# Adding four partial sums of squares on VectorE before the variance product, in two of four layer norms

## The chip, the cores and the metric

One NeuronCore of one Trainium2 chip runs the whole kernel. The metric is the device time of one execution, in microseconds (us), and a kernel is judged by the median of its runs. TensorE (PE in the profile) multiplies matrices, VectorE (DVE) and ScalarE (ACT) do elementwise work, GpSimd (POOL) and SyncE (SP) issue the data transfers (DMA) here.

## The reference

The kernel computes a trunk of two layers on an input of 512 tokens by 1024 features, all in float32. Layer 0 mixes tokens by a state-space group and an attention group; layer 1 by a convolution. Each layer ends as follows:

```python
x = layer_norm(DEEPNORM_ALPHA * x + mix, ln1_g[layer], ln1_b[layer])
ffn = sqrelu_mlp(x, ffn_w1[layer], ffn_b1[layer], ffn_w2[layer], ffn_b2[layer])
x = layer_norm(DEEPNORM_ALPHA * x + ffn, ln2_g[layer], ln2_b[layer])
```

A layer norm takes, for each token, the mean of its 1024 features and the mean of the squared differences from it:

```python
mu = jnp.mean(xf, axis=-1, keepdims=True)
var = jnp.mean(jnp.square(xf - mu), axis=-1, keepdims=True)
y = (xf - mu) * lax.rsqrt(var + LN_EPS)
```

The convolution of layer 1 has a further layer norm inside it.

## The kernel before

**Layout.** The activations lie transposed: features on the 128 partitions, tokens along the free dimension. The 1024 features make eight tiles (`KT = 8`) of 128 x 512. A product in nearly full float32 precision is made of three matmuls on split operands: each tensor is kept as a high part and a low part (`whi` and `wlo` for weights, `xbh` and `xbl` for the activations behind norm "b"), and `gemm` (its matmuls are recorded as L256) multiplies high by high, high by low and low by high for each of eight tiles, so 24 matmuls make one output tile.

**The layer norms.** Four norms are made in this way: "a" behind the mixer of layer 0, "b" behind the first FFN, "c" inside the convolution, "d" behind the convolution. (The last norm of the kernel is made differently.) Each works on two halves of the tokens, 256 columns each, since `HALVES` is (0, 256) and (256, 512). Since the features lie on partitions, a sum over features crosses partitions; TensorE does that in `colmean`, by a matmul whose stationary operand is the constant tile `ones` (recorded as L954). Its operands are plain float32. `centre` subtracts the mean from the eight tiles (VectorE, L385), squares them (ScalarE, L185) into eight tiles `sq`, and adds neighbours on VectorE (L385), so that four partial sums are left; `scale` passes these four to `colmean`, which accumulates four matmuls in one PSUM tile, named `vpb` for norm "b" and `vpd` for norm "d" (`mpb` and `mpd` hold the mean). `rsqrt` then takes the reciprocal square root on ScalarE (L191) and improves it in three VectorE operations (`tb`, `tb`, `rb`). `ln_to_x` multiplies each tile by the result and splits it into `xbh` and `xbl`.

**What covers the norms.** `tail_norm_lead` interleaves the norm with other products so that TensorE has work. The tail is the last product before the norm, eight output tiles for each half (PSUM tiles `tlb`, `tld`). The lead is the first product behind the norm (PSUM tiles `pl` behind norm "b" and `fl` behind norm "d"). By `BEFORE = (1, 3, 1, 2)`, the first half has one tail tile of the second half ahead of its mean product and three more ahead of its variance product; the second half has one lead tile (on the first half's result) ahead of its mean product and two more ahead of its variance product. Behind norm "b" the lead has four tiles, behind norm "d" six. When the lead has been made on the first half, `Lead.finish` makes it on the second half, which needs the second half's `xbh` and `xbl`.

**What sets the order.** The Tile framework's scheduler places instructions from the program's order and its own costs; `colmean` uses `tc.issue_after(last)`, so that its matmuls are placed behind the last matmul of the covering product. On each engine the instructions then run strictly in that order. Weights of the leads come from DRAM copies that were kept earlier (`kepth`, `keptl`), loaded by DMAs that GpSimd issues.

Of the kernel before, what the change touches and what calls it, by code (L numbers as in the profile page):

```python
# [13 lines left out]
ALU = mybir.AluOpType  # L14
# [29 lines left out]
LEAD = 6  # L44
TOGETHER = {'fl1': 2}
LN_ON_V = "abcd"
KEEP_FROM = 8
AHEAD = (5, 4)
FJ = 3
# [109 lines left out]
def units_of(name, w, k0, nk, cols, width):  # L159

    ncol = 1024 // nk
    out = []
    for c in cols:
        base = c // width * width
        src = w[k0 * P : (k0 + nk) * P, base : base + width].rearrange("(k p) n -> p k n", p=P)
        out.append(((name, k0, base), src, nk, ncol, c - base, width))
    return out
# [29 lines left out]
def kernel(ctx: ExitStack, tc: tile.TileContext, a: dict, out: bass.AP):  # L197
# [186 lines left out]
    def tt(o, x, y, op):  # L384
        V.tensor_tensor(o, x, y, op=op)  # L385
        return o
# [493 lines left out]
    def tmp(name, dt=F32):  # L880
        return hid.tile([P, T], dt, tag="tmp", name=name, bufs=8)
# [14 lines left out]
    for layer in range(2):  # L896
# [4 lines left out]
        for nb in FFN_BLOCKS[layer]:  # L901
# [11 lines left out]
            for m in range(k0, k0 + nb, 4):  # L913
                units += units_of("f10", a["ffn_w1"][0], 0, 8, range(m * P, min(m + 4, k0 + nb) * P, 128), 256)
                if m >= KEEP_FROM:
                    keep_at["f", m + 3] = kept[n : n + 2]
# [14 lines left out]
    class LN:  # L931
# [29 lines left out]
        def centre(self, ys, c0, c1, other=None):  # L961

            mu = self.colmean([self.s[c0]], c0, c1, "m", other)
            sq = []
            for j, y in enumerate(ys):
                tt(y[:, c0:c1], y[:, c0:c1], mu, ALU.subtract)
                sq.append(tmp(f"sq{self.n}{c0}{j}")[:, c0:c1])
                act(sq[j], y[:, c0:c1], AF.Square)
            for j in range(0, KT, 2):
                tt(sq[j], sq[j], sq[j + 1], ALU.add)  # L970
            return sq[::2]

        def scale(self, sq, c0, c1, other=None):
            var = self.colmean(sq, c0, c1, "v", other)
# [531 lines left out]
```

## Time and profile before

| what | value |
|---|---|
| median of 3 runs | 1173.91 us (1172.56 to 1175.39) |
| the profiled execution | 1172.98 us |
| its span, first to last instruction | 1171.2 us |
| mean granted TensorE clock | 0.993 |
| TensorE busy with matmuls | 1138.9 us (97%) |
| VectorE busy | 822.9 us (70%) |
| ScalarE busy | 551.7 us (47%) |

Norm "b" lies at about 597 to 639 us of the span, norm "d" at about 788 to 831 us. One float32 matmul of `colmean` is recorded as two matmul instructions, so a variance product of four shows as "x8". Busy times of TensorE overlap, because a matmul is recorded until its last result is out while the next has begun; what a group of matmuls takes is read from the chain of waits, which follows back from the last instruction what released each piece of work and counts no time twice.

### The profile page before, as it was taken

Reading aid. Unit: us, or ns where it says so; the run is one execution under the profiler, and the core shown is the slowest. Engines: PE = TensorE matmul, PEld = TensorE weight load, DVE = VectorE, ACT = ScalarE, POOL = GpSimd, SP = SyncE. Lnnn points to the kernel's source line nnn. Section 1 sums busy time; section 2 is a strip of 40 time slices with the busy share of each in tenths; the row PEclk is TensorE's granted clock in tenths of the full one; section 3 lists DMA queues with packets and bytes.
Section 4 is the critical chain, followed back from the end, with each engine's and each line's share of the span. In section 5 each row is a group of like instructions: output and inputs, shape, how many; then the busy total and the mean of one; then the engine's idle time right before and its main releaser. Section 6 shows DMA issues by size and latency. Waiting matters only on the chain.

```text
span 1171.2 us, 17896 instructions
## 1 busy us (share of the span) xinstructions
PE 1138.9 (97%) x7180; PEld 953.1 (81%) x7180; DVE 822.9 (70%) x1396; ACT 551.7 (47%) x838; POOL 67.0 (6%) x125
## 2 busy tenths in 40 slices
PE   9989999999999999999999999899989999999997
PEld 7777767799888888888999777599968888887885
DVE  7999875498646546546555899886785958587337
ACT  7857779345425425425323132662753536363530
POOL 1022210000000000000021110001000000000000
PEclk9999999999999999999999999999989999999999
DMA  8521221332688788788454742206324151514211
GB/s 216 165 56 50 79 85 46 110 116 73 221 286 289 250 287 290 249 286 286 164 177 152 247 144 74 75 9 209 91 79 138 56 151 37 170 36 153 63 55 72
DMA packets 145907, 169.59 MB, mean 145 GB/s; under 512 B 13922, under 2 KB 119138, under 8 KB 145824
## 3 DMA queue, kind: packets, MB, share of 16 engines
q1 hardware_dynamic: 137024, 136.96, 36.7%
q0 software_dynamic: 8640, 31.46, 7.9%
q8 instruction: 56, 0.92, 0.3%
q14 instruction: 27, 0.22, 0.1%
q10 hardware_dynamic: 160, 0.03, 0.0%
HBM read 132.12 MB, written 35.65 MB: 143 GB/s over the span
## 4 chain that ended last, share of the span: by engine, by line
PE 82%; DVE 9%; ACT 4%; issue 2%; DMA 2%; POOL 0%; SPq 0%; DVEq 0%; ACTq 0%; POOLq 0%
PE f L256 24%; PE acf L256 11%; PE s L1390 8%; PE fl L256 5%; PE tlb L256 4%; PE tld L256 4%; PE h L1436 4%; PE pv L256 3%; PE pg L256 3%; PE cw L1165 3%; PE tla L256 2%; PE acmo L256 2%; PE pl L256 2%; DVE wlo L111 1%; PE gg L256 1%
## 5 line engine op out<-in xcount | busy, mean ns | idle before, releaser
L110 ACT CAST whi<-raw 128x1024 fp32r<-128x1024 f32 (+1 forms) x150 | 156.7, 1061 | 257.9 <-PE acf L256 61.0
L111 DVE TENSOR_TENSOR wlo<-raw,whi 128x1024 fp32r<-128x1024 f32 (+1 forms) x150 | 183.8, 1238 | 123.9 <-ACT whi L110 120.5
L256 PE MATMUL f<-xdh,whi 128*128 128x512 f32 x208 | 81.0, 390 | 1.0 <-ACT whi L110 1.0
L256 PE MATMUL f<-xah,whi 128*128 128x512 f32 x208 | 81.1, 390 | 0.0
L256 PE MATMUL f<-xal,whi 128*128 128x512 f32 x208 | 80.9, 389 | 0.0
L256 PE MATMUL f<-xah,wlo 128*128 128x512 f32 x208 | 80.9, 389 | 0.0
L256 PE MATMUL f<-xdl,whi 128*128 128x512 f32 x208 | 80.9, 389 | 0.0
L256 PE MATMUL f<-xdh,wlo 128*128 128x512 f32 x208 | 80.9, 389 | 0.0
L256 PE MATMUL acf<-hh,whi 128*128 128x512 f32 x192 | 75.4, 392 | 0.0
L256 PE MATMUL acf<-hh,wlo 128*128 128x512 f32 x192 | 75.2, 392 | 0.0
L256 PE MATMUL acf<-hl,whi 128*128 128x512 f32 x192 | 74.8, 390 | 0.0
L1390 PE MATMUL s<-whi,ah 128*128 128x512 f32 x168 | 66.0, 400 | 3.3 <-ACT whi L110 2.5
L1390 PE MATMUL s<-wlo,ah 128*128 128x512 f32 x168 | 66.4, 402 | 2.3 <-DVE wlo L111 2.3
L1390 PE MATMUL s<-whi,al 128*128 128x512 f32 x168 | 66.0, 396 | 0.0
L111 DVE TENSOR_TENSOR wlo<-quad,whi 128x1536 fp32r<-128x1536 f32 x28 | 49.0, 1754 | 4.7 <-ACT whi L110 4.4
L110 ACT CAST whi<-quad 128x1536 fp32r<-128x1536 f32 x28 | 41.0, 1478 | 21.9 <-PE f L256 8.0
L389 DVE SCALAR_TENSOR_TENSOR cy<-hp,wdw,cy 128x512 f32<-128x512 f32 (+1 forms) x75 | 49.5, 660 | 0.2 <-ACT cy L185 0.2
L95 POOL DMA_DIRECT2D whi<-kepth x30 | 16.1, 536 | 547.7 <-PE tlb L256 385.5
L256 PEld LDWEIGHTS f<-xdh,whi 128*128 128x128 f32 x208 | 39.0, 188 | 9.4 <-ACT whi L110 1.4
L256 PEld LDWEIGHTS f<-xah,whi 128*128 128x128 f32 x208 | 39.0, 188 | 8.2
L256 PEld LDWEIGHTS f<-xdh,wlo 128*128 128x128 f32 x208 | 39.0, 188 | 8.2
L256 PEld LDWEIGHTS f<-xah,wlo 128*128 128x128 f32 x208 | 39.0, 188 | 8.1
(649 smaller groups left out, 3069.1 us busy)
## 6 DMA issues: line engine op xcount, KB each, us to landing
raw<-in_ffn_w_dram SPq DMA_DIRECT2D x35, 1024.0 KB, 5.6
kepth<-whi SPq DMA_DIRECT2D x30, 512.0 KB, 3.4
keptl<-wlo SPq DMA_DIRECT2D x30, 512.0 KB, 9.4
whi<-kepth POOLq DMA_DIRECT2D x30, 512.0 KB, 3.6
wlo<-keptl POOLq DMA_DIRECT2D x30, 512.0 KB, 4.6
raw<-in_ffn_w_dram SPq DMA_DIRECT2D x28, 512.0 KB, 4.1
raw<-in_conv_w_pw_dram SPq DMA_DIRECT2D x12, 1024.0 KB, 7.3
quad<-in_ffn_w_dram SPq DMA_DIRECT2D x16, 768.0 KB, 4.8
```

The costliest lines, as they stand in the source:

```text
L95: nc.gpsimd.dma_start(x, d)
L110: i0 = nc.scalar.copy(hi, raw).ins
L111: i1 = nc.vector.tensor_sub(lo, raw, hi.bitcast(F32)).ins
L256: ins = PE.matmul(ps[:, c0:c1], u[:, k, ksl], v[:, c0:c1], start=start and k == 0 and i == 0, stop=stop and k == n - 1 and i == 2).ins
L389: V.scalar_tensor_tensor(o, x, s, y, op0=op0, op1=op1)
L1165: PE.matmul(cps[j, c0][g][C, :], Ds[j][t // 16][R, t % 16, :], hps[j][R, t + c0 : t + c1], start=t < 4, stop=t >= n - 4, tile_position=(R. ...
L1390: PE.matmul(ps, u, v[:, p, :], start=chain == i and p == 0 and n_ == 0, stop=p == len(As) - 1 and n_ == 2, skip_group_check=True)
L1436: PE.matmul(ps, u, v, start=k == 0 and i == 0, stop=k == nb_last - 1 and i == 2)
```

## The change

In norms "b" and "d", as each later neighbour sum is made, it is also added into the first one. One partial sum is left in place of four, and `colmean` gets a list of one, so the variance product is one float32 matmul in place of four. Norms "a" and "c" stay as they are.

```diff
+ONE_SUM = "bd"
...
             for j in range(0, KT, 2):
                 tt(sq[j], sq[j], sq[j + 1], ALU.add)
-            return sq[::2]
+                if self.n in ONE_SUM and j:
+                    tt(sq[0], sq[0], sq[j], ALU.add)
+            return sq[:1] if self.n in ONE_SUM else sq[::2]
```

There are two norms with two halves each, so TensorE has twelve float32 matmuls fewer and VectorE has twelve additions of 128 x 256 more. On ScalarE, GpSimd and SyncE the order of the instructions is the same as before. The line numbers of the changed kernel are larger by one to three.

TensorE, second half of norm "b", before: `pl2` and `pl3` are the third and fourth lead tiles, `vpb256` the variance product of the half that begins at column 256, `sqb2560` to `sqb2566` its four partial sums.

```order
L256 MATMUL pl2_5962<-xbh7_5599,whi124_5357 128x256
L256 MATMUL pl2_5962<-xbl7_5600,whi124_5357 128x256
L256 MATMUL pl2_5962<-xbh7_5599,wlo124_5358 128x256
L954 MATMUL vpb256_5987<-sqb2560_5910,ones_75 128x256
L954 MATMUL vpb256_5987<-sqb2562_5916,ones_75 128x256
L954 MATMUL vpb256_5987<-sqb2564_5922,ones_75 128x256
L954 MATMUL vpb256_5987<-sqb2566_5928,ones_75 128x256
L256 MATMUL pl3_6022<-xbh0_5585,whi125_5361 128x256
L256 MATMUL pl3_6022<-xbl0_5586,whi125_5361 128x256
```

The same place on TensorE in the changed kernel:

```order
L257 MATMUL pl2_5965<-xbh7_5599,whi124_5357 128x256
L257 MATMUL pl2_5965<-xbl7_5600,whi124_5357 128x256
L257 MATMUL pl2_5965<-xbh7_5599,wlo124_5358 128x256
L257 MATMUL pl3_6022<-xbh0_5585,whi125_5361 128x256
L955 MATMUL vpb256_5990<-sqb2560_5910,ones_75 128x256
L257 MATMUL pl3_6022<-xbl0_5586,whi125_5361 128x256
L257 MATMUL pl3_6022<-xbh0_5585,wlo125_5362 128x256
```

Three of the four matmuls with `ones` are gone, and the one that is left stands behind the first matmul of the fourth lead tile instead of ahead of it. The second half of norm "d" has the same two differences, with `fl` for `pl`. In the first halves three of the four are gone too, and nothing else on TensorE moves.

VectorE, first half of norm "b", before: `sqb00` to `sqb07` are the eight tiles of squares, `tlb2561` a tail tile of the second half, `X1` the activations that it is added to.

```order
L385 TENSOR_TENSOR sqb00_5630<-sqb00_5630,sqb01_5633 128x256
L385 TENSOR_TENSOR sqb02_5636<-sqb02_5636,sqb03_5639 128x256
L385 TENSOR_TENSOR sqb04_5642<-sqb04_5642,sqb05_5645 128x256
L385 TENSOR_TENSOR sqb06_5648<-sqb06_5648,sqb07_5651 128x256
L389 SCALAR_TENSOR_TENSOR X1_62<-tlb2561_5657,rb1_2541,X1_62 128x256
L385 TENSOR_TENSOR sb256_5683<-X0_61,X1_62 128x256
```

The same place on VectorE in the changed kernel:

```order
L386 TENSOR_TENSOR sqb00_5630<-sqb00_5630,sqb01_5633 128x256
L386 TENSOR_TENSOR sqb02_5636<-sqb02_5636,sqb03_5639 128x256
L386 TENSOR_TENSOR sqb04_5642<-sqb04_5642,sqb05_5645 128x256
L386 TENSOR_TENSOR sqb00_5630<-sqb00_5630,sqb02_5636 128x256
L386 TENSOR_TENSOR sqb06_5648<-sqb06_5648,sqb07_5651 128x256
L386 TENSOR_TENSOR sqb00_5630<-sqb00_5630,sqb04_5642 128x256
L390 SCALAR_TENSOR_TENSOR X1_62<-tlb2561_5660,rb1_2541,X1_62 128x256
L386 TENSOR_TENSOR sqb00_5630<-sqb00_5630,sqb06_5648 128x256
L386 TENSOR_TENSOR sb256_5686<-X0_61,X1_62 128x256
```

Three additions into `sqb00` have come in, and the last of them, on which the variance product waits, stands behind the addition of a tail tile. Norm "d" has the same in its first half.

VectorE, second half of norm "b", in the changed kernel (before, the first, second, third and fifth of these rows stood here alone, followed by the last):

```order
L386 TENSOR_TENSOR sqb2560_5910<-sqb2560_5910,sqb2561_5913 128x256
L386 TENSOR_TENSOR sqb2562_5916<-sqb2562_5916,sqb2563_5919 128x256
L386 TENSOR_TENSOR sqb2564_5922<-sqb2564_5922,sqb2565_5925 128x256
L386 TENSOR_TENSOR sqb2560_5910<-sqb2560_5910,sqb2562_5916 128x256
L386 TENSOR_TENSOR sqb2566_5928<-sqb2566_5928,sqb2567_5931 128x256
L386 TENSOR_TENSOR sqb2560_5910<-sqb2560_5910,sqb2564_5922 128x256
L386 TENSOR_TENSOR sqb2560_5910<-sqb2560_5910,sqb2566_5928 128x256
L390 SCALAR_TENSOR_TENSOR tb256_5993<-vpb256_5990,rb256_5992 128x256
```

Here nothing stands between the seven additions; only the last of them reads what the one just ahead of it has written.

## The prediction

> **What bounds the kernel now.** The page comes first. It gives, by rows, TensorE's and VectorE's busy time with share and instructions, and then the shares of the chain of waits that ended last.
>
> ```profile
> PE 1138.9 (97%) x7180; PEld 953.1 (81%) x7180; DVE 822.9 (70%) x1396; ACT 551.7 (47%) x838; POOL 67.0 (6%) x125
> PE 82%; DVE 9%; ACT 4%; issue 2%; DMA 2%; POOL 0%; SPq 0%; DVEq 0%; ACTq 0%; POOLq 0%
> ```
>
> TensorE carries 82% of the chain, VectorE 9%, but a share over the whole span does not decide about four short places. So the second view is the chain itself around norm "b" (start, duration in us, what).
>
> ```profile
> 597.54 8.56 PE tlb L256 x72
> 606.10 1.73 PE vpb L954 x8
> 607.83 11.41 PE tlb L256 x96
> 619.23 2.88 PE pl L256 x24
> 622.11 0.43 PE mpb L954 x2
> 622.54 5.75 PE pl L256 x48
> 628.29 1.74 PE vpb L954 x8
> 630.03 0.02 issue
> 630.06 0.48 ACT rb L191
> ...
> 632.98 0.04 issue
> 633.03 0.74 PE pl L256 x4
> ```
>
> TensorE goes from the tail through the variance product to the tail and the lead without a pause; both variance products are links of the chain. Behind the second one the chain leaves TensorE for 3.00 us (630.03 to 633.03, through ScalarE and VectorE) and comes back to it. The same view around norm "d":
>
> ```profile
> 797.49 1.73 PE vpd L954 x8
> ...
> 819.78 1.73 PE vpd L954 x8
> 821.51 8.63 PE fl L256 x72
> ```
>
> Here TensorE has 8.63 us of lead tiles behind the second variance product, so the norm's own chain, 3.00 us long in "b", is covered. VectorE's sums of squares are in neither piece of the chain. At all four places TensorE is what comes last.
>
> **What is removed.** A float32 matmul is two recorded instructions; four of them take 1.73 or 1.74 us in the chain, and the mean product of one matmul takes 0.43 us (622.11). One left of four therefore saves 1.30 us, at four places 5.2 us. The chain counts nothing twice, so this is the price I take.
>
> **What is added on VectorE.** VectorE's timeline in both halves of norm "b", with the variance products (TensorE) that its sums must reach in time:
>
> ```profile
> 600.24 1.43 DVE L385 TENSOR_TENSOR sqb<-sqb,sqb 128x256 f32<-128x256 f32 x4
> 601.58 0.48 DVE L389 SCALAR_TENSOR_TENSOR X<-tlb,rb,X 128x256 f32<-128x256 f32 x1
> 602.09 0.42 DVE L385 TENSOR_TENSOR sb<-X,X 128x256 f32<-128x256 f32 x1
> 605.94 0.38 PE L954 MATMUL vpb<-sqb,ones 128*128 128x256 f32 x1
> 608.37 0.42 DVE L389 SCALAR_TENSOR_TENSOR tb<-vpb,rb 128x256 f32<-128x256 f32 x1 [1.29 <-ACT rb L191]
> 625.24 1.43 DVE L385 TENSOR_TENSOR sqb<-sqb,sqb 128x256 f32<-128x256 f32 x4
> 628.13 1.89 PE L954 MATMUL vpb<-sqb,ones 128*128 128x256 f32 x8
> 630.56 0.43 DVE L389 SCALAR_TENSOR_TENSOR tb<-vpb,rb 128x256 f32<-128x256 f32 x1 [3.90 <-ACT rb L191]
> 631.02 0.42 DVE L385 TENSOR_TENSOR tb<-tb,rb 128x256 f32<-128x256 f32 x1
> ```
>
> The product's rows of 0.38 us for one instruction and 1.89 us for eight show that its instructions overlap, so 6 x 0.38 = 2.3 us would overstate what goes.
>
> Four independent additions take 1.43 us and the last of them 0.42, so one follows another after (1.43 - 0.42) / 3 = 0.34 us. An operation that reads what the one just ahead wrote starts 0.46 us after it (630.56 to 631.02). In the second half the seventh addition is the only one of that kind: it starts 5 x 0.34 + 0.46 = 2.16 us behind the first and ends 0.42 later, at 625.24 + 2.58 = 627.82 us. TensorE gets to the variance product at 628.13 plus one lead matmul that now stands ahead of it: 72 of them take 8.63 us, so 0.12, which makes 628.25. About 0.4 us is left over, and the wait is nothing. That cover is thin: its name is the second and third lead tile (48 matmuls, 5.75 us). The price of the additions has two bounds. None of them can go faster than 0.34 us, so below nothing they can't go: there is no gain in them. If all seven followed at 0.46 us, the last would end at 625.24 + 6 x 0.46 + 0.42 = 628.42 us and TensorE would wait 0.2 us. I take zero, since the order shows just one dependent neighbour, and keep 0.2 us for the range.
>
> In the first half the last sum also stands behind the addition of a tail tile. That one waited for nothing at 601.58 (no bracket on its row), so its tile is ready by then. The sum comes out at 600.24 + 5 x 0.34 + 0.34 + 0.51 + 0.42 = 603.2 us, where 0.51 is from 601.58 to 602.09. TensorE arrives at 605.94: 2.7 us of cover, given by three tail tiles (72 matmuls, 8.56 us). Behind it VectorE was idle for 1.29 us before `tb`, which waits for the norm itself. What is queued behind the new additions, the tail's additions, is thus pushed by at most 1.2 us into gaps. Norm "d" is alike:
>
> ```profile
> 791.56 1.42 DVE L385 TENSOR_TENSOR sqd<-sqd,sqd 128x256 f32<-128x256 f32 x4
> 797.33 0.38 PE L954 MATMUL vpd<-sqd,ones 128*128 128x256 f32 x1
> 816.73 1.43 DVE L385 TENSOR_TENSOR sqd<-sqd,sqd 128x256 f32<-128x256 f32 x4
> 819.62 1.89 PE L954 MATMUL vpd<-sqd,ones 128*128 128x256 f32 x8
> ```
>
> From sums to product there are 5.77 us in the first half (3.0 needed) and 2.89 + 0.12 in the second (2.58 needed).
>
> [...]
>
> **What moves.** In both second halves the first matmul of the fourth lead tile now stands ahead of the variance product. It needs a weight that GpSimd loads; that wait stood right behind the product before, and TensorE did not stop there (next matmul after 1.74 us of chain). In "d" the move costs nothing, for 8.63 us of lead cover 3.00. In "b" the chain of 3.00 us bounds what follows: one row of the waits shows TensorE's weight load stopped for it.
>
> ```profile
> PEld pl L256 <- ACT xbh L185: 0.3, 1, 0.3
> ```
>
> With one lead matmul fewer behind the product, this wait grows from 0.3 to 0.4 us. So the second half of "b" gives 1.30 - 0.12 = 1.18 us.
>
> **The sum.** 3 x 1.30 + 1.18 = 5.1 us. Against the profiled execution (1172.98 us, of which 1171.2 are the span and 1.8 lie around it) this makes 1167.9 us. The median of the runs is 0.9 us above that execution; the same step gives 1173.91 - 5.1 = 1168.8 us, which is my forecast.
>
> **Does it reach the end?** Two later stretches could swallow it. Windows of the convolution (busy us of each engine in each stretch), and the pieces behind "d":
>
> ```profile
> 640.00:660.00 20.00, 20.00 (x110) 17.40 (x109) 12.39 (x21) 4.60 (x7) 5.75 (x11) 1.00 0.91 315
> 680.00:700.00 20.00, 20.00 (x92) 15.62 (x92) 19.73 (x33) 4.42 (x7) 3.38 (x7) 1.00 0.57 195
> 737.51 2.14 issue
> 835.90 11.54 PE fl L256 x96
> 847.43 0.02 issue
> 847.46 0.70 ACT r L185
> SPq L124 <- PE fl L1051: 40.4, 1, 40.4
> 850.00:860.00 10.00, 7.10 (x27) 5.21 (x27) 8.07 (x7) 7.85 (x12) 0.00 (x0) 0.83 0.00 0
> ```
>
> VectorE (third busy figure) is full from 680 us on, so the convolution may be its bound; but from 640 to 660 it has 12.39 of 20 us and waits for TensorE's products, so its full stretch begins when TensorE delivers and moves along with it. Behind "d" the chain goes from TensorE's last lead tile into ScalarE at 847.46. The weights there (the transfer of L124) are issued when TensorE's `fl` of L1051 lets their buffer go, so they move too. I see nothing that stands still.
>
> **Rivals.**
> - *Given back later.* If VectorE's load or a transfer holds the convolution and the FFN at their old times, the two norms' 2.5 and 2.6 us turn into waits, and the time is 1173.9 us, or about 1171.4 when only one is kept. For it: the 19.73 of 20 us. Against it: the two starts named above. Chance 0.11, of which 0.03 is half kept.
> - *The variance product waits for the sums,* and the kernel is slower. Place: the second halves of both norms, where TensorE runs in order and the rest of the lead is queued behind the product, VectorE's `tb` behind that. If an added sum costs a us, TensorE waits 3a - 1.6 us at each (the four old ones end at 625.24 + 1.43 = 626.67, and from there to 628.25 are 1.6). The gain is eaten when 2 x (3a - 1.6) = 5.1, at a = 1.4 us; at a = 1.8 the time is 1168.8 + 7.6 = 1176.4 us. For it: a chain through one buffer, each sum waiting for the one ahead. Against it: 0.46 us for such a pair in the trace. Chance 0.06, most of it slower.
> - *Lost clock.* The granted clock (third figure from the end) is 0.83 from 850 to 860 us, where TensorE has gaps: 0.17 x 10 = 1.7 us at most. A shift by 5 us moves the work against whatever times these drops; one more or fewer is 1.7 us, and the stop of 2.14 us without a releaser at 737.51 may come or go alike. Both widen the forecast and don't replace it. [...]
>
> That the change does not do what it says is excluded by the order: twelve matmuls are gone.
>
> **Chances and range.** The forecast has 0.83, nearly all of it faster. 0.2% of 1173.91 is 2.3 us, about what a measurement of this kernel can tell from no change; so faster means below 1171.6 us. Faster: 0.81 + 0.03 = 0.84. Same: 0.02 of the forecast's edge, 0.08 given back, 0.02 of late sums, together 0.12. Slower: 0.04. The low end takes one clock drop or stop away and some of the runs' spread (1168.8 - 3.0 = 1165.8); the high end adds both sums' waits (0.4), one drop (1.7) and half given back, not all at once: 1172.0.
>
> **What would show it.** The chain with 0.43 us at `vpb` and `vpd` in place of 1.73, at each of four places; no idle of TensorE before them that VectorE's `sqb` or `sqd` ends; the wait for `xbh` in "b" near 0.4 us; from "d" to the end the same distance as before. I am wrong if TensorE waits for `sqb` by more than 0.2 us, if the stretch between the norms is longer than before by what "b" gained, or if the pieces behind 847 us keep their absolute times.

## The result, and the profile after

The changed kernel takes 1170.92 us in the median of 13 runs (1167.43 to 1173.42), the kernel before 1175.3 us in 13 runs beside it (1169.41 to 1178.28). The ratio is 0.9967 with a 95% interval of 0.9957 to 0.9978, which of 1175.3 us is 3.9 us less, between 2.6 and 5.1. The profiled execution of the changed kernel took 1170.82 us, 2.2 us less than that of before. So the forecast of 5.1 us is at the upper end of what the first runs show, and above what the two profiles show. Where do the others go? First the three rows of the page of the changed kernel that answer to those of before: the span, the busy times, and the shares of the chain that ended last.

```profile
span 1169.1 us, 17858 instructions
PE 1137.3 (97%) x7156; PEld 949.2 (81%) x7156; DVE 826.8 (71%) x1408; ACT 551.8 (47%) x838; POOL 66.8 (6%) x125
PE 77%; DVE 5%; ACT 3%; issue 2%; DMA 1%; POOL 0%; SPq 0%; DVEq 0%; ACTq 0%
```

TensorE has 24 recorded matmul instructions fewer (twelve matmuls) and VectorE 12 more; the change did what it says. Its busy times are of no more help here. The chain of waits is: the changed kernel around norm "b" (start, duration in us, what).

```profile
598.20 0.43 PE mpb L955 x2
598.63 8.55 PE tlb L257 x72
607.18 0.43 PE vpb L955 x2
607.62 11.41 PE tlb L257 x96
...
622.34 5.87 PE pl L257 x49
628.21 0.45 PE vpb L955 x2
...
631.64 0.74 PE pl L257 x4
...
643.69 5.24 PE pv L257 x23
```

The two rows of the kernel before that bound the same stretch:

```profile
597.11 0.43 PE mpb L954 x2
...
645.09 5.24 PE pv L256 x23
```

Both variance products are down from 1.73 to 0.43 and 0.45 us, and the matmuls around them are as long as they were: 8.55 us for 72, 11.41 for 96. The stretch from the first mean product to `pv` was 645.09 - 597.11 = 47.98 us and is 643.69 - 598.20 = 45.49: 2.49 less. Norm "d" of the changed kernel in the same view, down to the first piece behind it, and the one row of before that has not been shown yet:

```profile
789.10 0.43 PE mpd L955 x2
...
798.16 0.43 PE vpd L955 x2
...
819.28 0.43 PE vpd L955 x2
...
845.54 0.70 ACT r L186
```
```profile
788.43 0.43 PE mpd L954 x2
```

From mean product to ScalarE's `r` it was 847.46 - 788.43 = 59.03 us and is 56.44: 2.59 less. The two norms together give 5.08 us. VectorE's timeline of the changed kernel, first and second half of norm "b":

```profile
601.33 2.10 DVE L386 TENSOR_TENSOR sqb<-sqb,sqb 128x256 f32<-128x256 f32 x6
603.34 0.48 DVE L390 SCALAR_TENSOR_TENSOR X<-tlb,rb,X 128x256 f32<-128x256 f32 x1
603.73 0.42 DVE L386 TENSOR_TENSOR sqb<-sqb,sqb 128x256 f32<-128x256 f32 x1
...
625.03 2.56 DVE L386 TENSOR_TENSOR sqb<-sqb,sqb 128x256 f32<-128x256 f32 x7
629.18 0.42 DVE L390 SCALAR_TENSOR_TENSOR tb<-vpb,rb 128x256 f32<-128x256 f32 x1 [1.59 <-ACT rb L192]
```

TensorE's timeline where the second half's product starts, and the wait behind it:

```profile
628.04 0.59 PE L955 MATMUL vpb<-sqb,ones 128*128 128x256 f32 x2
```
```profile
PEld pl L257 <- ACT xbh L186: 0.5, 1, 0.5
```

In the second half the seven additions end at 625.03 + 2.56 = 627.59 us, and TensorE comes at 628.04, with no bracket on its row: 0.45 us to spare. In the first half the last sum is out at 604.15, 3 us ahead of the product at 607.18. The one wait that grows is that of the lead's weight load for `xbh`, from 0.3 to 0.5 us.

**Where the rest of the profiled difference went.** The table cuts both executions at the same instructions: at the first mean product of "b", "c" and "d", at the last lead matmul of "b" (0.12 us ahead of the first `pv`) and at the first matmul behind the last lead tile of "d" (0.20 us ahead of `r`). Each stretch is the difference of two starts in TensorE's timeline, where a matmul that follows another starts some 0.16 us earlier than its row of the chain.

| stretch, us | before | changed | difference |
|---|---|---|---|
| up to norm "b" | 596.95 | 598.04 | +1.09 |
| norm "b" | 47.85 | 45.37 | -2.48 |
| convolution | 100.16 | 102.22 | +2.06 |
| norm "c" | 43.31 | 43.31 | 0.00 |
| norm "d" | 58.99 | 56.40 | -2.59 |
| behind it | 323.99 | 323.75 | -0.24 |

The first stretch has the same instructions in both kernels, so its 1.09 us can't come from the change; the execution of the changed kernel has one drop of the clock more in it (0.76 in the window from 155 to 162 us, where it is 1.00 before). The convolution's 2.06 us might: it lies right behind norm "b". Windows of the changed kernel, then of before (us, busy us of TensorE, weight load, VectorE, ScalarE and GpSimd, and the granted clock third from the end):

```profile
725.00:745.00 20.00, 17.61 (x492) 11.23 (x484) 18.64 (x45) 5.30 (x12) 1.05 (x2) 0.91 0.17 56
740.00:743.50 3.50, 3.04 (x40) 1.05 (x18) 2.31 (x7) 2.08 (x6) 0.00 (x0) 0.52 0.03 7
```
```profile
725.00:745.00 20.00, 17.40 (x517) 11.13 (x499) 19.38 (x46) 5.20 (x12) 1.06 (x2) 1.00 0.17 57
```

TensorE's timeline in the convolution, changed and before:

```profile
672.16 1.06 PE L1168 MATMUL cw<-hp,D 32*32 32x512 f32 x6 [0.44 <-issue]
...
739.53 1.76 PE L1168 MATMUL cw<-hp,D 32*32 32x256 f32 x43 [1.93 <-issue]
```
```profile
739.65 1.41 PE L1165 MATMUL cw<-hp,D 32*32 32x256 f32 x55 [2.14 <-issue]
```

Two things are worse in this execution of the changed kernel: the clock is at about half for some 3.4 us from 740.1 on (0.52 in that window; 0.09 x 20 = 1.8 us lost in the stretch), and TensorE stops for 0.44 us at 672.16 without a releaser. The long stop of about 2 us is in both. The experiments ask whether these come with the change or with the execution.

### The profile page after: what moved, and what is told of

It is laid out like the page before. It is cut to its first block, busy times and chain, and to the rows that moved or that the text cites. A ratio compares the mean times of both kernels' runs of the same rounds, so it can differ in the third digit from the quotient of the medians.

```text
span 1169.1 us, 17858 instructions
## 1 busy us (share of the span) xinstructions
PE 1137.3 (97%) x7156; PEld 949.2 (81%) x7156; DVE 826.8 (71%) x1408; ACT 551.8 (47%) x838; POOL 66.8 (6%) x125
## 4 chain that ended last, share of the span: by engine, by line
PE 77%; DVE 5%; ACT 3%; issue 2%; DMA 1%; POOL 0%; SPq 0%; DVEq 0%; ACTq 0%
PE f L257 22%; PE acf L257 11%; PE s L1393 8%; PE fl L257 5%; PE tlb L257 4%; PE tld L257 4%; PE h L1439 4%; PE pv L257 3%; PE cw L1168 3%; PE pg L257 3%; PE pl L257 2%; DVE wlo L112 2%; PE acmo L257 1%; PE gg L257 1%; PE gv L257 1%
## 5 line engine op out<-in xcount | busy, mean ns | idle before, releaser
L257 PEld LDWEIGHTS f<-xal,whi 128*128 128x128 f32 x208 | 39.1, 188 | 8.1
```

What stands on the lines that cost most here:

```text
L257: ins = PE.matmul(ps[:, c0:c1], u[:, k, ksl], v[:, c0:c1], start=start and k == 0 and i == 0, stop=stop and k == n - 1 and i == 2).ins
```

## The experiments

The theory that stands: the four products' gain is whole, and what the convolution lost is a drop of the clock and a short stop that fall in some executions of either kernel. Rival one: VectorE is full in the convolution and swallows what "b" gains. Rival two: the place of the stops, and so the lost clock, depends on how many instructions TensorE has run, so that the loss comes with the change each time. Rival three: the added sums cost something, and the gain is that much smaller than the products' own. In the texts below "b" runs to its last lead matmul and "d" to its end, as in the table above (47.85 and 58.99 us before). The first text takes the convolution from rows of the chain, where it has 99.94 us before and 102.01 in the changed kernel.

**The kernel before once more.** No edit.

> The kernel before, unchanged, for a second profile. Three theories on the 2.07 us by which the convolution (from the first gate product behind norm b to the mean product of norm c) came out longer in the changed kernel, 102.01 us for 99.94. F (instructions): TensorE stops for lack of instructions in the small 32x32 products, and where it stops depends on how many TensorE instructions lie ahead of them; here, with the old count, the stretch is 99.9 us within 0.4 apart from clock drops, and there is no stop of TensorE near 672 us. C (chance): the stretch differs by 1 to 2 us between executions of one kernel. V (VectorE sets the pace of the convolution): 99.9 us again.

One run of 1176.39 us. "b" took 47.85 and "d" 58.99 us, to the hundredth as before; the convolution took 102.64 instead of 100.16. A window of it (same columns as above):

```profile
746.50:750.00 3.50, 3.50 (x73) 1.72 (x72) 2.13 (x6) 1.96 (x6) 0.00 (x0) 0.51 0.01 2
```

So the unchanged kernel can have the half clock there too, and its TensorE stopped for 0.27 us at 676.82 besides. The loss that looked like an answer to the change comes without it. The second rival falls in the form that the change brings it.

**Each norm alone.**

```diff
-ONE_SUM = "bd"
+ONE_SUM = "b"
```

> One sum in norm b alone, 6 float32 matmuls fewer. Norm b itself saves 2.5 us in all theories. F: the stop near 672 us is there (about 1.3 us lost), so 1.2 us faster than before, ratio about 0.9990. C: nothing is lost on average, 2.5 us faster, ratio about 0.9979. V: the convolution gives nearly all of it back, 0 to 0.4 us faster, ratio 0.9997 to 1.

1174.3 us against 1176.99, ratio 0.9979 (0.9957 to 1.0001). "b" 45.39, "d" 58.99 and the convolution 100.50 us, with no drop of the clock in it and no stop near 672 us. VectorE gave nothing back here: the convolution of 100.16 us before became 100.50, while "b" gave 2.46. The runs agree in sign and size (2.5 us of 1177, 5.1 less to none), but their interval touches one.

```diff
-ONE_SUM = "bd"
+ONE_SUM = "d"
```

> One sum in norm d alone. It lies behind the convolution, so all three theories expect 2.6 us, ratio about 0.9978, with norm b as before. F and V: the convolution takes 99.9 us as before, with no stop near 672 us; C: it differs by 1 to 2 us.

1173.79 us against 1176.99, ratio 0.9973 (0.9953 to 0.9992), 3.2 us less. "d" 56.40 and "b" 47.85 us; the convolution 101.61 us, with a drop of the clock in it, though nothing ahead of it was changed. That speaks against both rivals that put the convolution's loss down to "b".

**The count of instructions kept, the work gone.** Three matmuls of two columns ahead of each variance product of "b", so that TensorE's count is that of before up to norm "d".

```diff
+PADDED = "b"
...
+                for _ in range(3 if nm == "v" and self.n in PADDED else 0):
+                    PE.matmul(ps[:, :2], ones, ones[:, :2], start=True, stop=True)
```

> The changed kernel, with three float32 matmuls of two columns on the constant tile put ahead of each variance product of norm b (their result is overwritten). TensorE has as many instructions ahead of the convolution as before, for a cost that no run shows yet, at most 0.4 us a half by an estimate from the 0.06 us of the smallest matmul spacing. F: the convolution is back at 99.9 us without a stop near 672 us, and the time is 5.1 less the padding (0.3 to 0.8 us) below before: ratio about 0.9961. C: the same total on average, the convolution anywhere within 2 us. V: the convolution gives back what b gained, 2.6 us faster in all, ratio 0.9978.

1173.52 us against 1176.99, ratio 0.996 (0.9941 to 0.9979). "b" 46.58, "d" 56.40 us, the convolution 102.41 with a drop at 747.1 and a stop of 0.32 us at 677.66. With the old count of instructions the long convolution is there as well, so the second rival falls from the other side too. The padding cost 1.2 us, 0.6 in each half, and not the 0.4 that was expected. The chain of this kernel shows it:

```profile
611.71 0.56 PE vpb L956 x6
612.27 0.54 PE vpb L958 x2
```

A matmul of two columns in float32 takes 0.19 us here, almost half of what one of 256 takes.

**The changed kernel once more.** No edit.

> The changed kernel again, for a second profile and a tighter ratio. Theory: the norms alone decide, 5.1 us, ratio about 0.9957, and the rest of the span differs from execution to execution by clock drops and stops of TensorE for instructions; from the first mean product of norm b to the last lead matmul 45.4 us, in norm d 56.4 us. Rival (part of it is given back in the convolution each time): 3.8 us, ratio 0.9968, the convolution 1 us or more above 100.2 us though no clock drop falls into it.

1172.16 us against 1177.46, ratio 0.9956 (0.9937 to 0.9975), 5.2 us less (2.9 to 7.4). "b" 45.37 and "d" 56.40 us again, and the convolution 100.41 us, a quarter of a us from the 100.16 of before. TensorE's timeline in the convolution, and the two rows of the chain that bound "b":

```profile
742.65 1.31 PE L1168 MATMUL cw<-hp,D 32*32 32x256 f32 x43 [2.12 <-issue]
```
```profile
602.25 0.43 PE mpb L955 x2
...
647.74 5.24 PE pv L257 x23
```

The same 43 matmuls took 1.31 us behind the same stop, where they took 1.76 in the first execution. By this execution the first rival falls: with the whole change the convolution is as long as before when no drop falls into it. How far one execution can be trusted there is taken up behind the experiments, since the convolution also varies without a drop.

**The products alone.** The sums into the first tile are left out.

```diff
             for j in range(0, KT, 2):
                 tt(sq[j], sq[j], sq[j + 1], ALU.add)
-                if self.n in ONE_SUM and j:
-                    tt(sq[0], sq[0], sq[j], ALU.add)
             return sq[:1] if self.n in ONE_SUM else sq[::2]
```

> The variance product takes the first partial sum alone and no sums are added on VectorE, so three quarters of the squares are left out of the variance in norms b and d. The order puts the product ahead of the fourth lead tile again. Theory: the added sums cost nothing, so norm d is 56.4 us as in the changed kernel, and norm b is 45.25, the 0.12 us shorter that the moved matmul cost. Rival (the added sums hold TensorE up by some tenths that the changed kernel hides): 0.2 us or more shorter in either norm.

One run of 1168.91 us; "b" 45.25, "d" 56.40 us. Without the added sums "b" is 0.12 us shorter and "d" not at all. The 0.12 is the one lead matmul: without the sums the product stands ahead of it again, behind 48 lead matmuls instead of 49, and TensorE's 48 end at 627.73 us in this chain. The convolution took 101.01 us with the clock whole.

**The sums alone.** All four matmuls stay, over the one sum.

```diff
-            return sq[:1] if self.n in ONE_SUM else sq[::2]
+            return [sq[0]] * 4 if self.n in ONE_SUM else sq[::2]
```

> The sums are added as in the changed kernel, but four matmuls are made of the total, so the variance is four times too large in norms b and d. Theory: VectorE's twelve additions are free, so norm d is 59.0 us as before and norm b 47.97, as before with one matmul fewer behind the product (0.12). Rival (additions cost time): each norm up to 1 us longer than that.

One run of 1177.54 us; "b" 47.97, "d" 58.99 us. The chain and VectorE's timeline of this kernel:

```profile
609.33 1.73 PE vpb L955 x8
...
631.64 1.74 PE vpb L955 x8
```
```profile
628.47 2.55 DVE L386 TENSOR_TENSOR sqb<-sqb,sqb 128x256 f32<-128x256 f32 x7
```

Seven additions end at 631.02, and TensorE's timeline has the product's start at 631.48, 0.46 us later. The price of all twelve additions is the 0.12 us of the lead matmul in "b". The third rival falls: the whole gain is the products', 1.30 each. The convolution took 101.46 us with the clock whole, although "b" gained nothing here.

**Where the cover ends.** Each added sum gets one more VectorE operation ahead of it that changes nothing in the numbers.

```diff
                 if self.n in ONE_SUM and j:
+                    tt(sq[j], sq[j], sq[j], ALU.max)
                     tt(sq[0], sq[0], sq[j], ALU.add)
```

> The changed kernel with one more VectorE operation in front of each added sum (the maximum of the partial sum with itself, which changes nothing). The order puts the variance product of the second halves behind nine matmuls of the fourth lead tile in place of one. The sums then end about 1 us later, at 628.8 on the clock of before, and TensorE arrives at 629.2, so it does not wait for them. Theory: the norm's own chain of 3.0 us behind the product has 8 matmuls less to hide behind in norm b, 8 x 0.12 = 0.96 us, which makes 46.3 us; in norm d the three lead tiles still cover it, 56.4 us. Rival (only the sums' end counts, not what stands behind the product): both norms alike, 45.4 and 56.4 us.

One run of 1176.92 us; "b" 46.33, "d" 56.40 us. The chain in the second half of "b", and two rows of the waits:

```profile
627.59 6.83 PE pl L257 x57
634.42 0.45 PE vpb L955 x2
```
```profile
PEld pl L257 <- ACT xbh L186: 1.4, 1, 1.4
PE pl L257 <- ACT xbh L186: 1.2, 1, 1.2
```

Ten VectorE operations instead of seven moved the product behind nine lead matmuls in place of one. TensorE did not wait for the sums. It waited afterwards, because eight matmuls fewer were left to cover the norm's 3 us chain: "b" lost 0.96 us of its gain, and "d", with 7.55 us of lead still behind its product, lost nothing. Late sums are paid on the far side of the product.

**The third norm as well.**

```diff
-ONE_SUM = "bd"
+ONE_SUM = "abd"
```

> One sum in norm a too (with b and d as in the changed kernel). In norm a the sums have less cover: the order puts the variance product behind 62 matmuls of the tail in place of 42 in the first half, and behind 50 of tail and lead in place of 32 in the second. From the first mean product of norm a to the last lead matmul before took 48.84 us. Theory (TensorE loses only what the norm's chain no longer hides): 2 x 1.30 saved, less at most 1.1 us in the first half, where the product now ends 20 x 0.12 - 1.30 us later than before and the lead waits for its result; 46.2 to 47.3 us, ratio to before about 0.994. Rival (a later product costs what it is late, in both halves): 2.6 - 1.1 - 0.9, so 48.2 us, ratio about 0.995.

1174.58 us against 1177.25, ratio 0.9973 (0.9948 to 0.9997). "b" 45.37 and "d" 56.40 us, but norm "a", from its first mean product to its last lead matmul, took 51.49 us where it was 48.84 before and 48.83 in the changed kernel. Neither expectation held. The chain of "a" in this kernel, its wait, and its clock:

```profile
254.65 2.01 DVE sqa L386 x6
...
261.35 0.52 ACT xah L186
...
261.91 0.62 PE fl L257 x3
...
276.32 0.45 PE vpa L955 x2
...
279.75 20.36 PE fl L257 x155
```
```profile
PE fl L257 <- ACT xah L186: 3.5, 2, 2.1
```
```profile
281.00:284.00 3.00, 3.00 (x18) 3.00 (x17) 3.00 (x9) 1.37 (x4) 0.00 (x0) 0.55 0.00 0
```

The sums of "a" stand on VectorE with the tail's additions between them, and from 253.66 us on VectorE is the chain. In the first half TensorE waits 1.42 us ahead of the lead. In the second the 3 us behind the product at 276.32 are covered by little, since 49 lead matmuls are used up ahead of the product where 31 were before, and 2.06 us remain. Behind that stop the clock stood at half for 3.4 us, which costs up to 1.7. Two products' 2.60 us against 3.48 of waits and 1.7 of clock make +2.6; measured are +2.65. That it closes so well is partly luck: the next kernel has the same two waits in "a" without a drop and takes 50.23 us there, so the drop is worth 1.26 us and the waits cost 3.99. The expectation had counted the lost cover for the first half alone; in the second, too, a lead that is spent ahead of the product is missing behind it.

**All four.**

```diff
-ONE_SUM = "bd"
+ONE_SUM = "abcd"
```

> One sum in norms a and c too. In norm c's first half TensorE waits for the sums already (0.31 us idle ahead of its variance product), with no product of its own to do: the last sum comes 2.56 - 1.43 = 1.13 us later and the product is 1.30 us shorter, but its first three matmuls ran beside the sums before. Theory: in the first half the product ends about 0.7 us later and ScalarE, which sets the pace there, starts 0.5 us later. In the second half the order puts the product behind 61 matmuls in place of 35, and what the norm's chain no longer hides is lost. From the mean product of norm c to that of norm d, 43.3 us before: 42.5 to 44.5 us. Rival (fewer matmuls always save): 40.7 us. Norm a as in the kernel with three norms; the total between 2 us slower and 1 us faster than that one.

1177.03 us against 1177.25, ratio 0.9991 (0.9973 to 1.0009): no difference that can be measured, and in the medians 2.5 us more than with three norms, where at most 2 were expected. "a" took 50.23 us, and "c" 46.18 instead of 43.31. A row of the waits and a window of the clock:

```profile
PE vpc L955 <- DVE sqc L386: 2.8, 1, 2.8
```
```profile
755.50:762.00 6.50, 5.99 (x126) 3.84 (x140) 5.04 (x13) 4.86 (x12) 0.00 (x0) 0.50 0.39 140
```

Here the prediction's losing rival stands in the open: in "c", behind a full VectorE, TensorE waits 2.8 us for the sums (0.3 in the changed kernel), and for 6.5 us from within that wait on the clock is at half. The 2.87 us are not all loss. The tail behind the first mean product of "d", in the chain of the changed kernel and then of this one:

```profile
789.53 8.63 PE tld L257 x72
```
```profile
796.44 6.35 PE tld L257 x53
```

Here 19 matmuls of the tail (2.28 us) stand ahead of that product which stood behind it, so they count in "c", and "d" is as much shorter: 54.12 us instead of 56.40. Without them "c" took 43.90 us, within the 42.5 to 44.5 that were expected, though neither a wait of 2.8 us nor the half clock was in that sum. "c" and "d" together take 100.30 us instead of 99.71: the 2.60 us that two products save are gone, and 0.59 more. The mean granted clock of its runs is 0.988, that of the kernel before beside it 0.991; 0.003 of 1177 us is 3.5 us. No version tried that takes the whole variance is faster than the changed kernel.

## Why the prediction was right

**The products.** 1.30 us each was the term, and 1.73 to 0.43 (0.45 in the second halves) is what the chain shows. With the products alone the norms were as short as with the sums, to within the one lead matmul, so the term is shown and not only read.

**The second half of "b".** 1.18 us was forecast for it, because the lead matmul that slips ahead takes away cover. "b" as a whole gave 2.49 us; 1.30 + 1.18 is 2.48. The wait for `xbh` came out at 0.5 us for a forecast 0.4.

**VectorE's sums.** Forecast were 2.58 us for seven and about 0.4 us to spare; measured are 2.56 and 0.45, and no wait of TensorE for `sqb` or `sqd`. With the sums alone the price was 0.12 us in "b" and none in "d". In the changed kernel, too, independent additions follow one another after 0.34 us: six of them take 2.10 us in the first half of "b" and one alone 0.42, and (2.10 - 0.42) / 5 is 0.34.

**The sum.** 5.1 us forecast. The two norms gave 2.49 + 2.59 = 5.08 in the profiles, the same to the hundredth in the second execution of the changed kernel. The runs gave 3.9 (2.6 to 5.1) and, measured again, 5.2 (2.9 to 7.4). Both intervals hold the forecast, the first at its end. The forecast time of 1168.8 us was 2.1 us too low. Of these, 1.4 are where it started from: it took the 5.1 us from the three runs shown, 1173.91, and with 13 runs the median of before is 1175.3. The other 0.7 are the step of the two medians, 4.4 in place of 5.1.

**Given back later.** It fell, but not by the first profile, where the stretch between the norms was 2.06 us longer, close to the sign of being wrong that the prediction had set. In the convolution VectorE is nearly as full as before (18.64 of 20 us from 725 on, 19.38 before), and the stretch varies without the change. With the clock whole it took 100.16 and 101.46 us in two executions without the gain of "b" in front of it, and 100.41, 100.50 and 101.01 in three with it. With a drop of the clock in it, it took 101.61 and 102.64 without the gain, and 100.94 to 102.41 in five with all or part of it. In neither group is it longer with the gain. Behind "d" it is 323.99 and 323.75 us; the second execution of the kernel before had 321.42 there.

**The product waits for the sums.** It didn't happen in "b" and "d", and the runs showed where it does: in "c" at once (2.8 us), in "a" behind the product rather than at it. In the second half of "b" three more operations on VectorE cost 0.96 us. The rival was put too narrowly, at the wait ahead of the product; the price is asked behind it first.

**Lost clock.** The prediction let it widen the range and had it right that one drop costs up to 1.7 us and comes or goes. The stop at 737.51, which it let come or go, came in all twelve executions. What it did not say is that the profile alone can then mislead: between the two first profiles 3 of the 5.1 us are hidden by drops and a short stop, 1.1 ahead of any change and 2.1 in the convolution.

## What to carry to other kernels

By what this kernel shows, a product of four float32 matmuls with a matrix of ones is worth summing first on VectorE if TensorE is the chain at that place and VectorE has the time: count the additions at 0.34 us, set their end against TensorE's arrival, and then count what is left to cover the chain *behind* the product, since a scheduler that lets other work go ahead takes it from there. A gain of 0.4% is read from a stretch of the trace that the change bounds, cut at the same instructions in both kernels, not from two spans: here the stretches of the two norms repeat to 0.02 us, the convolution only to 2.5 us, and the spans of one kernel differ by several us. A stretch that grew next to the change is first looked for in a second execution of the kernel before.

## What was not expected of the hardware

**The spread goes with the clock.** Among 29 runs of the kernel before on one chip the fastest took 1170.42 us at a mean granted clock of 0.996, the slowest 1182.84 at 0.986. 0.010 of 1177 us is 11.8, and the two are 12.4 apart; a straight line of time over clock takes up 81% of the variance of the 29. In the traces of the two first executions the clock is at 0.50 in each drop; ahead of the last, each lasts 3.41 us, one of them 6.83, and the drops begin a whole number of steps of 3.41 us apart (226, 5 and 86 before; 21, 171, 33 and 91 in the changed kernel). But drops aren't all that differs. The two executions of the changed kernel reach norm "b" at 598.04 and 602.09 us, and a row of TensorE's waits from 150 to 165 us, of the first execution and then of the second, shows a cause beside the clock, far ahead of the change (us in total, times, longest):

```profile
PE av L756 <- POOL w2C L705: 2.1, 2, 1.2
```
```profile
PE av L756 <- POOL w2C L705: 5.3, 2, 4.4
```

In the second comparison of the two kernels, a straight line through time over clock of all runs (17 and 12), with one step between the kernels, puts the change at 4.7 us less (3.6 to 5.8, two standard errors each way), a narrower interval than the medians give; for "b" alone it gives 1.2 (0.2 to 2.2) and for "d" alone 3.1 (2.3 to 3.9), less and more than the 2.5 and 2.6 us of the traces. Why these two stray I can't say; the clock is recorded to 0.001, which is 1.2 us.

**A drop can follow a stop of 2 us.** Behind 2.06 us without work in norm "a" (with three norms) and behind 1.93 us in the convolution (the changed kernel) a drop followed, behind 2.43 us there too (the kernel before once more); behind 2.14 us (before), 2.12 us (the changed kernel again) and 1.68 us ("b" alone) none did. So the length of the stop alone does not decide, and no run took a stop away to show that it brings the drop.

**Stops without a releaser.** In the convolution's 32x32 matmuls TensorE stopped for 1.6 to 2.4 us at one place in all twelve profiled executions, and for 0.3 or 0.4 us at another in four. The queue of instruction transfers has 56 of them in the page of the changed kernel, and one begins 2.0 us ahead of the short stop and one 0.3 us ahead of the long one (at 669.67 and 737.29 us). That TensorE has run out of instructions there would fit, but nine other transfers of the convolution have no such stop behind them, and no run here took the transfers away, so it stays open.
